# Making half of the modulated channels directly in the tile of token combinations, moving their hi/lo splits ahead of the first convolutions, and a third weight buffer in the modulation (trunk layer, float32, one core)

## The chip, the cores and the metric

The kernel runs on one core of a Trainium2 chip. The metric is the device time of one execution in microseconds (us), as the median of several runs; lower is better.

## The reference

One trunk layer on 128 prompt tokens and 512 sample tokens with 1024 channels, all float32: a modulated RMSNorm, two groups of attention heads, an output projection, a second modulated RMSNorm, and a ConvFFN with 2816 hidden channels in each of a gate and a value half. Modulation vectors come from `adaln`. What matters here is the part behind attention:

```python
sh1, sc1, gt1, sh2, sc2, gt2 = jnp.split(jax.nn.silu(cond) @ w_mod + b_mod, 6)
x = x + gt1 * rmsnorm(merge_heads(oa, ob, g_grp_a, g_grp_b, w_out), g_mix_post)
h = rmsnorm(x, g_ffn_pre) * (1 + sc2) + sh2          # modulate
u = h @ w_up                                          # 1024 -> 2 * 2816
u = up[:-2]*conv_w[0] + up[1:-1]*conv_w[1] + up[2:]*conv_w[2] + conv_b   # along tokens, zero padded
gate, val = jnp.split(u, 2)
x = x + gt2 * rmsnorm((silu(gate) * val) @ w_down, g_ffn_post)
```

## The kernel before

Float32 products are made from pairs of reduced values: every operand is split into a high part (a copy on ScalarE, `act`) and a low part (a subtraction, usually on VectorE), and `mm3` issues three matmuls for each pair of blocks. The names used below: PE is TensorE, DVE is VectorE, ACT is ScalarE, POOL is GpSimd, SP is the queue from which nearly all transfers are issued.

The kernel's instructions are issued in the order of the program text from the point on that this case is about (`manual_schedule`), each engine takes its own instructions strictly in that order, and semaphores hold an instruction until its inputs and its buffer are there. So an instruction that waits holds up everything behind it on its engine. Three stages matter.

**Projection and second norm (340 to 406 us).** Five token tiles t (t = 0 is the prompt) are projected in two halves (`p_mm`, PSUM tile `psyb`), added to the first head group (`p_y`), squared (`p_sq`), scaled by the gate (`p_z`: half 0 on POOL, half 1 on DVE), normed (`p_r`, `p_x`), squared again (`p_sx`, whose reciprocal root is two tiny POOL instructions, `rx1v` and `rx1r`), scaled (`p_n`, DVE, which makes `xn`), transposed on PE (`p_T`, PSUM `psh`), and modulated (`p_h`) into a float32 tile `hf` of 4 channel blocks by 128 tokens, one for each half `kb` of the channels; `p_s` splits it into `h2H` and `h2L`. Between them `tick` places eight small products for the last gate (`psada`, 16 matmuls each): `side_next` loads a 512 KB weight block `wms` for each, into one of two buffers (`WS`) that are used in turn. Then `up_mm(fi, gv, ch)` multiplies the hidden-channel blocks fi = 0 and 1 (gv: gate or value) with the first half of the tokens (`C1`, ch 0); `up_ev` copies the result out of PSUM into `raw`.

**Token combinations.** The later hidden blocks use a seven-product scheme over two halves of the tokens (C1, C2) and of the channels. It needs sums and differences of the modulated activations. Two tiles, `FG[0]` = F and `FG[1]` = G (both are called `fg` in the profile), are made by `fg(t)` on POOL: F = `h2H[0]` + `h2L[0]`, G = `h2H[1]` + `h2L[1]`, then G -= F. Later F and G are combined over the halves C1 and C2 on POOL and split by `t_hl` into `TF` and `TG` (`tf`, `tg` in the profile): ACT makes the high part and DVE the low part.

**Plain blocks and the unit loop (406 us on).** PSUM is handed over to four tiles of two banks: `zx` and `yy`, two buffers each. Blocks 0 and 1 get their second token half (`zz[0]`, `zz[1]`), blocks 2 and 3 are multiplied plainly (`plain`, with weights split by `plain_w`), `gate(0)` and `gate(1)` transpose the gate columns, `conv`, `silu` and `gate_mul` finish a block. Then `unit(u)` runs for u = 4 to 21, with seven products each; unit 4 needs the `zx` buffer that `conv(2, 0)` reads.

Lines of the helpers: L108 `act`, L111 `tt`, L120 `stt`, L127 `mm`; L371 `ada_mm`.

Of the kernel before, what the change touches and what calls it, by code (L numbers as in the profile page):

```python
# [15 lines left out]
KD = 8  # L16
# [10 lines left out]
def trunk_kernel(  # L27
# [46 lines left out]
    def U(shape, name, dt=F32):  # L74
        return up_.tile(shape, dt, tag="u", name=name)
# [8 lines left out]
    def PB(shape, name, dt=F32):  # L84
        return pp_.tile(shape, dt, tag="p", name=name)
# [18 lines left out]
    def f(ap):  # L104
        return ap.bitcast(F32)
# [4 lines left out]
    def tt(out, a, b, op, eng=None):  # L110
        return (eng or nc.vector).tensor_tensor(out=out, in0=a, in1=b, op=op)  # L111
# [1246 lines left out]
    def p_T(t):  # L1358
        for kb in range(2):
            pt = PS("t", "psh2")  # L1360
            hf = PB([128, 512], "h2f").rearrange("p (k t) -> p k t", k=4)
            hfs[t, kb] = pt, hf
            for kk in range(4):
                k = kb * 4 + kk
                nc.tensor.transpose(pt[:, kk * 128:kk * 128 + 128], xns[t][:, k * 128:k * 128 + 128], ident)
# [18 lines left out]
            act(h_, hv)  # L1384

    def fg_start():
        for kb in range(2):
            t_ = U([128, 4, 644], f"fg{kb}")
            FG.append(t_)
            for o, n in ((128, 1), (641, 3)):  # L1390
                nc.gpsimd.memset(t_[:, :, o:o + n], 0.0)

    def fg(t):

        c_ = slice(TO[t], TO[t] + 128)
        f_, g_ = (x[:, :, c_] for x in FG)
        for x, kb in ((f_, 0), (g_, 1)):
            tt(x, f(h2H[kb][:, :, c_]), f(h2L[kb][:, :, c_]), ALU.add, eng=nc.gpsimd)
        tt(g_, g_, f_, ALU.subtract, eng=nc.gpsimd)

    R = {}
# [89 lines left out]
    def side_next():  # L1491
        for x in sides:
            if x[1] is None:
                x[1] = WS([128, KD, 128], "wms")
                nc.sync.dma_start(
                    out=x[1], in_=wmod[:, x[0] * 128:x[0] * 128 + 128].rearrange("(k p) f -> p k f", p=128))
                return

    tn = [0]

    def tick():
        tn[0] += 1
# [8 lines left out]

    side_next()
    side_next()

    def p_hs(t):
        p_h(t, 0, range(4))
# [1 line left out]
        p_s(t, 0, 0)  # L1518
        p_s(t, 0, 1)

    p_mm(0, 0)
    p_y(0, 0)
    p_sq(0, 0)
    p_z(0, 0)
    for t in range(5):
# [33 lines left out]
        if t > 0:  # L1559
            p_hs(t - 1)  # L1560
            if t == 3:
                p_hl1(t - 1)
        p_sq(t + 1, 0)
        tick()
        p_sx(t)
        if t > 2:
            tick()
        p_z(t + 1, 0)
        if t == 2:
            load_x(4)  # L1570
    up_w(1, 0, True, 1)
# [17 lines left out]
    while act_sides:  # L1589
        tick()  # L1590
    r_load(2)
    fg_start()
    for t in range(3):
        fg(t)
    up_ev(0, 0, 0)
    p_T(4)
    p_hs(4)
    p_hl1(4)
    fg(3)
    p_s(4, 1, 1)  # L1600
    up_ev(0, 1, 0)
    up_mm(1, 1, 0)
    fg(4)
    up_ev(1, 0, 0)
    up_ev(1, 1, 0)
    r_load(3)

# [204 lines left out]
        up_mm(0, gv, 1, zz[0][:, (LS, RS)[gv]])  # L1812
    tt(F_[:, :, C2], F_[:, :, C2], F_[:, :, C1], ALU.subtract, eng=POOL)
    r_load(4)
    plain_w(2, 1)
    plain_w(3, 0)
    gate(0)
    for gv in range(2):
        up_mm(1, gv, 1, zz[1][:, (LS, RS)[gv]])
        up_ev(0, gv, 1)  # L1820
    t_hl(TG, G_, C2)
    tt(F_[:, :, C1], F_[:, :, C1], G_[:, :, C2], ALU.add, eng=POOL)
    tt(G_[:, :, C1], G_[:, :, C1], G_[:, :, C2], ALU.subtract, eng=POOL)
    for gv in (1, 0):
        conv(0, gv)
    plain(2, 0)
    for gv in range(2):
        up_ev(1, gv, 1)
    silu(0)
    gate_mul(0)  # L1830
    sums(4)
    plain_w(3, 1)
    r_load(5)
    t_hl(TF, F_, C2)
    for gv in (1, 0):
        conv(1, gv)
    gate(1)
    plain(2, 1)
    silu(1)
    gate_mul(1)  # L1840
    t_hl(TF, F_, C1)
    plain(3, 0)
    sums(5)
    t_hl(TG, G_, C1)
    a_hi(4)
    a_lo(4)
    r_load(6)
    sa_hi(4)
    sa_lo(4)
    conv(2, 0)  # L1850
    conv(2, 1)
    silu(2)
    gate_mul(2)
# [146 lines left out]
```

## Time and profile before

| | |
|---|---|
| median of 3 runs | 848.97 us |
| the 3 runs | 848.97, 855.26, 848.74 us |
| the profiled execution, its own time | 855.52 us |
| its span, first to last instruction | 853.6 us |
| PE busy / weight load busy | 806.5 us (94%) / 708.5 us (83%) |
| DVE, ACT, POOL busy | 564.7, 436.0, 303.2 us |
| mean granted PE clock | 0.976 |
| transfers | 106.59 MB, mean 125 GB/s |

All times of rows are microseconds from the start of the span. PE carries the kernel, so what is read from the profile is where PE does not work (its waits and what ended them) and where it works at a lower granted clock. Both can be seen in views of the trace: the waits of PE by what released them, the instructions of an engine in order of time, and tables of short stretches with each engine's busy time, the granted clock (PEclk, 1.00 is full) and the transfers' share. The profiled execution is 6.55 us slower than the median run.

### The profile page before, as it was taken

Reading aid. Unit: us, or ns where it says so; the run is one execution under the profiler, and the core shown is the slowest. Engines: PE = TensorE matmul, PEld = TensorE weight load, DVE = VectorE, ACT = ScalarE, POOL = GpSimd, SP = SyncE. Lnnn points to the kernel's source line nnn. Section 1 sums busy time; section 2 is a strip of 40 time slices with the busy share of each in tenths; the row PEclk is TensorE's granted clock in tenths of the full one; section 3 lists DMA queues with packets and bytes.
Section 4 is the critical chain, followed back from the end, with each engine's and each line's share of the span. In section 5 each row is a group of like instructions: output and inputs, shape, how many; then the busy total and the mean of one; then the engine's idle time right before and its main releaser. Section 6 shows DMA issues by size and latency. Waiting matters only on the chain.

```text
span 853.6 us, 13902 instructions
## 1 busy us (share of the span) xinstructions
PE 806.5 (94%) x5304; PEld 708.5 (83%) x5304; DVE 564.7 (66%) x1023; ACT 436.0 (51%) x876; POOL 303.2 (36%) x352
## 2 busy tenths in 40 slices
PE   6999989899999999989997999999999999999996
PEld 5679778788777777768997999999999987888885
DVE  3455555555888875676679899898898864332115
ACT  5345665645667886465445545546456544332112
POOL 3452333323221211346964466575575200000002
PEclk8999999999999999999998999999999999999999
DMA  9954535436312113567124243233332436434313
GB/s 290 277 142 127 155 97 142 122 105 164 86 50 75 50 51 104 197 207 196 42 65 128 83 129 110 87 115 104 107 115 84 125 114 221 171 110 161 114 50 124
DMA packets 140158, 106.59 MB, mean 125 GB/s; under 512 B 12560, under 2 KB 121388, under 8 KB 140092
## 3 DMA queue, kind: packets, MB, share of 16 engines
q1 hardware_dynamic: 139084, 105.05, 41.5%
q8 instruction: 42, 0.69, 0.4%
q10 hardware_dynamic: 1008, 0.66, 0.3%
q14 instruction: 24, 0.20, 0.1%
HBM read 92.53 MB, written 13.16 MB: 124 GB/s over the span
## 4 chain that ended last, share of the span: by engine, by line
PE 48%; DVE 28%; ACT 7%; DMA 5%; issue 4%; POOL 4%; SPq 1%; DVEq 0%; ACTq 0%; POOLq 0%
PE psd L127 16%; PE psg L127 8%; DVE cv L120 7%; DVE ou L111 5%; PE psv L127 4%; DVE cv L111 3%; DVE owl L111 3%; PE zx L127 3%; POOL fg L111 3%; PE psya L127 3%; PE psyb L127 2%; DMA wms<-in_w_mod_dram 2%; PE psS L127 2%; ACT cv L108 2%; DVE yy L111 2%
## 5 line engine op out<-in xcount | busy, mean ns | idle before, releaser
L127 PE MATMUL psd<-dwh,a 128*128 128x512 f32 x440 | 138.3, 395 | 0.0
L111 POOL TENSOR_TENSOR wsum<-wraw 128x512 f32<-128x512 f32 x36 | 77.2, 2166 | 96.9 <-DVE oc L111 89.1
L127 PE MATMUL zx<-h2H,ou 128*128 128x322 f32 x392 | 96.7, 316 | 7.5 <-DVE cv L120 4.4
L127 PEld LDWEIGHTS psd<-dwh,a 128*128 128x128 f32 x440 | 82.9, 188 | 19.7
L127 PE MATMUL psd<-dwl,a 128*128 128x512 f32 x220 | 87.1, 396 | 0.1
L111 DVE TENSOR_TENSOR dwl<-wd,dwh 128x1024 fp32r<-128x1024 f32 x22 | 26.9, 1224 | 86.7 <-ACT dwh L108 86.7
L127 PE MATMUL psg<-hH,wh 128*128 128x320 f32 x224 | 76.0, 339 | 4.4 <-ACT T L108 4.2
L127 PEld LDWEIGHTS zx<-h2H,ou 128*128 128x128 f32 x392 | 69.0, 192 | 9.9 <-DVE yy L111 5.2
L127 PE MATMUL psg<-hH,wl 128*128 128x320 f32 x224 | 70.5, 315 | 0.0
L127 PE MATMUL psg<-hL,wh 128*128 128x320 f32 x224 | 70.3, 314 | 0.0
L108 ACT ACTIVATE dwh<-wd 128x1024 fp32r<-128x1024 f32 x22 | 23.3, 1060 | 91.4 <-PE psd L127 85.7
L117 POOL TENSOR_SCALAR rdv<-ssdc 128x1 f32<-128x1 f32 x5 | 1.6, 329 | 177.3 <-ACT jk L108 177.3
L127 PE MATMUL zx<-h2L,ou 128*128 128x322 f32 x196 | 61.4, 313 | 0.0
L127 PEld LDWEIGHTS psg<-hH,wh 128*128 128x128 f32 x224 | 42.8, 191 | 13.2 <-ACT T L108 7.9
L108 ACT ACTIVATE cv<-yy,T 128x642 f32<-128x642 f32 x20 | 17.7, 886 | 66.1 <-DVE yy L111 66.1
L127 PEld LDWEIGHTS psd<-dwl,a 128*128 128x128 f32 x220 | 41.3, 188 | 10.4 <-DVE dwl L111 0.6
L111 POOL TENSOR_TENSOR wl<-wst,wh 128x1024 fp32r<-128x1024 f32 (+1 forms) x12 | 27.7, 2311 | 58.5 <-ACT wh L108 41.7
L120 DVE SCALAR_TENSOR_TENSOR cv<-yy,T,cv 128x641 f32<-128x641 f32 x40 | 35.4, 884 | 17.9 <-ACT cv L108 17.2
L108 ACT ACTIVATE P<-P,nm 128x320 f32<-128x320 f32 (+3 forms) x64 | 40.3, 630 | 7.0 <-DVE nm L626 6.9
L127 PEld LDWEIGHTS psg<-hL,wh 128*128 128x128 f32 x224 | 43.1, 192 | 0.5
L127 PEld LDWEIGHTS psg<-hH,wl 128*128 128x128 f32 x224 | 42.9, 192 | 0.0
L108 ACT ACTIVATE cv<-cv 128x642 f32<-128x642 f32 x22 | 16.4, 744 | 50.2 <-DVE cv L120 50.2
(354 smaller groups left out, 2248.0 us busy)
## 6 DMA issues: line engine op xcount, KB each, us to landing
wraw<-in_w_up_dram SPq DMA_DIRECT2D x40, 512.0 KB
wms<-in_w_mod_dram SPq DMA_DIRECT2D x32, 512.0 KB
wd<-in_w_down_dram SPq DMA_DIRECT2D x22, 512.0 KB
wm<-in_w_mod_dram SPq DMA_DIRECT2D x16, 512.0 KB
aD<-cv SPq DMA_DIRECT2D x22, 321.0 KB
ar<-aD SPq DMA_DIRECT2D x11, 642.0 KB
wst<-in_w_in_dram SPq DMA_DIRECT2D x10, 512.0 KB
yD<-Y SPq DMA_DIRECT2D x5, 512.0 KB
```

The lines of the kernel that those rows point to most:

```text
L108: return nc.scalar.activation(out=out, in_=in_, func=func, **kw)
L111: return (eng or nc.vector).tensor_tensor(out=out, in0=a, in1=b, op=op)
L117: return e.tensor_scalar(out=out, in0=a, scalar1=s1, scalar2=s2, op0=op0, op1=op1)
L120: return nc.vector.scalar_tensor_tensor(out=out, in0=a, scalar=s, in1=b, op0=op0, op1=op1)
L127: return nc.tensor.matmul(out, l, r, start=start, stop=stop, skip_group_check=True, **kw)
```

## The change

1. `p_T` lets `p_h` write its result `hf` straight into F (for kb = 0, all five t) and into G (for kb = 1, t = 3 and 4, since G exists from there on). `fg(t)` then no longer makes F, and makes the sum for G only for t < 3. The subtraction G -= F stays for all five.
2. `fg_start` makes one tile at a time: F ahead of the first `p_mm`, G ahead of `p_T(3)`. `fg(0)` is issued behind `p_n(4)`, `fg(1)` to `fg(3)` where `fg(0)` to `fg(2)` were, `fg(4)` behind the last `p_s`.
3. Every third `wms` block goes to a third buffer, the first 1024 columns of `wmsk`, which is free by then; three blocks are loaded ahead instead of two.
4. `p_z(t + 1, 0)` (POOL) is issued ahead of `p_sx(t)`.
5. `up_ev(0, 1, 0)` and `up_ev(1, 0, 0)` are issued ahead of `p_T(4)` instead of behind the last `p_s`.
6. The four `t_hl` and two of the POOL combinations are issued earlier, `conv(2, 0)` ahead of `sums(5)` and the splits of unit 4's `OSA`, `plain_w(3, 1)` behind `conv(1, ...)`.

```diff
     def p_T(t):
         for kb in range(2):
             pt = PS("t", "psh2")
-            hf = PB([128, 512], "h2f").rearrange("p (k t) -> p k t", k=4)
+            if kb < len(FG):
+                hf = FG[kb][:, :, TO[t]:TO[t] + 128]
+            else:
+                hf = PB([128, 512], "h2f").rearrange("p (k t) -> p k t", k=4)
...
     def fg_start():
-        for kb in range(2):
-            t_ = U([128, 4, 644], f"fg{kb}")
-            FG.append(t_)
...
+        t_ = U([128, 4, 644], f"fg{len(FG)}")
+        FG.append(t_)
...
     def fg(t):
...
-        for x, kb in ((f_, 0), (g_, 1)):
-            tt(x, f(h2H[kb][:, :, c_]), f(h2L[kb][:, :, c_]), ALU.add, eng=nc.gpsimd)
+        if t < 3:
+            tt(g_, f(h2H[1][:, :, c_]), f(h2L[1][:, :, c_]), ALU.add, eng=nc.gpsimd)
         tt(g_, g_, f_, ALU.subtract, eng=nc.gpsimd)
...
-                x[1] = WS([128, KD, 128], "wms")
+                sn[0] += 1
+
+                x[1] = (wmsk[:, 0:1024].rearrange("p (k f) -> p k f", k=KD) if sn[0] % 3 == 0
+                        else WS([128, KD, 128], "wms"))
...
     side_next()
     side_next()
+    side_next()
...
+    fg_start()
     p_mm(0, 0)
...
         p_sq(t + 1, 0)
+        p_z(t + 1, 0)
         tick()
         p_sx(t)
         if t > 2:
             tick()
-        p_z(t + 1, 0)
...
+    fg_start()
     p_T(3)
     p_n(4)
+    fg(0)
...
-    fg_start()
-    for t in range(3):
+    for t in range(1, 4):
         fg(t)
     up_ev(0, 0, 0)
+    up_ev(0, 1, 0)
+    up_ev(1, 0, 0)
     p_T(4)
     p_hs(4)
     p_hl1(4)
-    fg(3)
     p_s(4, 1, 1)
-    up_ev(0, 1, 0)
+    fg(4)
     up_mm(1, 1, 0)
-    fg(4)
-    up_ev(1, 0, 0)
     up_ev(1, 1, 0)
...
     r_load(4)
+    t_hl(TG, G_, C2)
     plain_w(2, 1)
+    tt(F_[:, :, C1], F_[:, :, C1], G_[:, :, C2], ALU.add, eng=POOL)
+    tt(G_[:, :, C1], G_[:, :, C1], G_[:, :, C2], ALU.subtract, eng=POOL)
+    t_hl(TF, F_, C2)
     plain_w(3, 0)
...
-    t_hl(TG, G_, C2)
-    tt(F_[:, :, C1], F_[:, :, C1], G_[:, :, C2], ALU.add, eng=POOL)
-    tt(G_[:, :, C1], G_[:, :, C1], G_[:, :, C2], ALU.subtract, eng=POOL)
     for gv in (1, 0):
         conv(0, gv)
+    t_hl(TF, F_, C1)
     plain(2, 0)
...
-    plain_w(3, 1)
     r_load(5)
-    t_hl(TF, F_, C2)
+    t_hl(TG, G_, C1)
     for gv in (1, 0):
         conv(1, gv)
+    plain_w(3, 1)
...
-    t_hl(TF, F_, C1)
-    plain(3, 0)
-    sums(5)
-    t_hl(TG, G_, C1)
     a_hi(4)
     a_lo(4)
+    plain(3, 0)
+    conv(2, 0)
+    sums(5)
     r_load(6)
     sa_hi(4)
     sa_lo(4)
-    conv(2, 0)
     conv(2, 1)
```

PE's own sequence is the same in both kernels, word for word, except that the third and the sixth of the eight `psada` groups read `wmsk`. The other engines' sequences change at these places.

On SP, from the second to the last of the `wms` loads (`xr` are the residual inputs, `yD` is where the normed rows are parked):

```order
-L1495 DMA wms<-in_w_mod_dram 128x8x128
+L1501 DMA wms<-in_w_mod_dram 128x8x128
+L1501 DMA wmsk<-in_w_mod_dram 128x8x128
 L1351 DMA yD<-Y_3916 128x1024
-L1495 DMA wms<-in_w_mod_dram 128x8x128 x2
+L1501 DMA wms<-in_w_mod_dram 128x8x128 x2
 L1351 DMA yD<-Y_3916 128x1024
-L1495 DMA wms<-in_w_mod_dram 128x8x128
+L1501 DMA wmsk<-in_w_mod_dram 128x8x128
 L1303 DMA xr<-in_x_sample_dram 128x1024
-L1495 DMA wms<-in_w_mod_dram 128x8x128
+L1501 DMA wms<-in_w_mod_dram 128x8x128
```

The third load now stands ahead of the first `yD`, and from there on each load waits for the `psada` group three before its own, instead of two before.

On ACT, at the hand-over of PSUM to `zx` and `yy`, from the first copy out of `psu` to the first weight split of the plain blocks, before:

```order
L108 ACTIVATE raw<-psu 128x322
L108 ACTIVATE h2f<-psh_5070,S_104,G_103 128x128 x4
L108 ACTIVATE h2H_4437<-h2f 128x4x128
L108 ACTIVATE h2f<-psh_5076,S_104,G_103 128x128 x2
L108 ACTIVATE h2H_4438<-h2f 128x4x128
L108 ACTIVATE raw<-psu 128x322
L108 ACTIVATE raw_5127<-psu 128x322 x2
L108 ACTIVATE ou<-wraw 128x1024
L108 ACTIVATE pwh<-wraw 128x1024
```

and in the changed kernel (`fg_4496` is F, `fg_4987` is G):

```order
L108 ACTIVATE raw<-psu 128x322 x2
L108 ACTIVATE raw_5063<-psu 128x322
L108 ACTIVATE fg_4496<-psh_5065,S_104,G_103 128x128 x4
L108 ACTIVATE h2H_4437<-fg_4496 128x4x128
L108 ACTIVATE fg_4987<-psh_5070,S_104,G_103 128x128 x2
L108 ACTIVATE h2H_4438<-fg_4987 128x4x128
L108 ACTIVATE raw_5063<-psu 128x322
L108 ACTIVATE ou<-wraw 128x1024
L108 ACTIVATE tg_5129<-fg_4987 128x4x322
L108 ACTIVATE pwh<-wraw 128x1024
```

One copy instead of three stands behind the last modulation, and the first split of G stands ahead of `pwh`.

On DVE, up to the convolution of block 2 that stands ahead of unit 4 (`cv<-raw` are the convolutions of blocks 0 and 1, `cv<-zx` is `conv(2, 0)`, `ou` and `owl` are splits of unit 4's weights), before:

```order
L111 TENSOR_TENSOR tg_5146<-fg_5056,tg_5145 128x4x322
L120 SCALAR_TENSOR_TENSOR cv<-raw,T_99,cv 128x641 x4
L111 TENSOR_TENSOR cv<-cv 128x642
L111 TENSOR_TENSOR pwl<-wraw,pwh 128x1024
L111 TENSOR_TENSOR tf_5144<-fg_5053,tf_5143 128x4x322
L120 SCALAR_TENSOR_TENSOR cv<-raw_5127,T_99,cv 128x641 x4
L111 TENSOR_TENSOR cv<-cv 128x642
L111 TENSOR_TENSOR tf_5144<-fg_5053,tf_5143 128x4x322
L111 TENSOR_TENSOR tg_5146<-fg_5056,tg_5145 128x4x322
L111 TENSOR_TENSOR ou<-wraw,ou 128x1024
L111 TENSOR_TENSOR owl<-wsum,owh 128x1024
L120 SCALAR_TENSOR_TENSOR cv<-zx,T_99,cv 128x641 x2
```

and in the changed kernel, where the first split of G (`tg`) stands right ahead of the first of these rows:

```order
L111 TENSOR_TENSOR pwl<-wraw,pwh 128x1024
L111 TENSOR_TENSOR tf_5128<-fg_4496,tf_5127 128x4x322
L111 TENSOR_TENSOR pws<-wraw,pws 128x1024
L120 SCALAR_TENSOR_TENSOR cv<-raw,T_99,cv 128x641 x4
L111 TENSOR_TENSOR tf_5128<-fg_4496,tf_5127 128x4x322
L111 TENSOR_TENSOR cv<-cv 128x642
L111 TENSOR_TENSOR tg_5130<-fg_4987,tg_5129 128x4x322
L120 SCALAR_TENSOR_TENSOR cv<-raw_5063,T_99,cv 128x641 x4
L111 TENSOR_TENSOR pwl<-wraw,pwh 128x1024
L111 TENSOR_TENSOR cv<-cv 128x642
L111 TENSOR_TENSOR ou<-wraw,ou 128x1024
L120 SCALAR_TENSOR_TENSOR cv<-zx,T_99,cv 128x641 x2
```

The splits of F and G that stood right ahead of unit 4's weights now stand among the convolutions of blocks 0 and 1, and between those and `conv(2, 0)` only two weight splits and a product are left.

More of the change, by code (lines that the diff above doesn't have):

```diff
@@ L1386, in fg_start @@
     def fg_start():
-        for kb in range(2):
-            t_ = U([128, 4, 644], f"fg{kb}")
-            FG.append(t_)
-            for o, n in ((128, 1), (641, 3)):
-                nc.gpsimd.memset(t_[:, :, o:o + n], 0.0)
+        t_ = U([128, 4, 644], f"fg{len(FG)}")
+        FG.append(t_)
+        for o, n in ((128, 1), (641, 3)):
+            nc.gpsimd.memset(t_[:, :, o:o + n], 0.0)
     def fg(t):
@@ L1497, in side_next @@
                 return
-    tn = [0]
+    tn, sn = [0], [0]
     def tick():
```

## The prediction

> **What bounds the kernel now.** I read the page first, and its first part says where to look:
>
> ```profile
> PE 806.5 (94%) x5304; PEld 708.5 (83%) x5304; DVE 564.7 (66%) x1023; ACT 436.0 (51%) x876; POOL 303.2 (36%) x352
> ```
>
> PE is the bound, and PE's own sequence of instructions does not change. So the change can only be worth what PE waits, or runs at a reduced clock, in the stretch that it touches. The view of PE's waits, asked for 330 to 460 us, has four rows in all:
>
> ```profile
> PE zx L127 <- DVE cv L120: 4.4, 1, 4.4
> PE psada L371 <- DMA wms<-in_w_mod_dram: 2.9, 1, 2.9
> PE zx L127 <- ACT raw L108: 2.2, 1, 2.2
> PE psh L1365 <- DVE xn L116: 1.7, 1, 1.7
> ```
>
> Together 11.2 us. The second thing is the clock. The table of short stretches shows it around these waits (the third number from the end is the granted clock):
>
> ```profile
> 355.00:359.00 4.00, 2.26 (x20) 1.56 (x22) 2.74 (x3) 0.86 (x4) 3.42 (x5) 1.00 0.02 4
> 379.00:380.00 1.00, 0.00 (x0) 0.00 (x0) 0.42 (x2) 1.00 (x3) 0.00 (x0) 0.92 1.02 295
> 386.00:387.00 1.00, 1.00 (x5) 0.80 (x4) 0.00 (x0) 0.00 (x0) 0.00 (x0) 0.66 0.00 0
> 407.00:408.00 1.00, 1.00 (x7) 1.00 (x6) 0.62 (x1) 0.35 (x1) 0.94 (x1) 0.58 1.15 288
> 410.00:411.00 1.00, 1.00 (x7) 1.00 (x6) 0.00 (x0) 0.00 (x0) 1.00 (x2) 0.72 0.00 0
> 454.00:455.00 1.00, 0.00 (x0) 0.00 (x0) 1.00 (x1) 0.00 (x0) 0.00 (x0) 0.97 0.14 39
> 461.00:462.00 1.00, 1.00 (x6) 1.00 (x5) 0.63 (x2) 1.00 (x2) 0.00 (x0) 0.62 0.22 82
> ```
>
> Between full speed and 0.50, a mean of 0.92 is 0.16 us at half, 0.66 is 0.68 us, and so on. So the clock was 0.50 from 379.84 to 386.68, from 407.16 to 410.56 and from 454.94 to 461.76: 6.84, 3.40 and 6.82 us, that is two, one and two pieces of some 3.41 us, and the starts lie 8 and 14 such pieces apart (27.32 and 47.78 us). The clock is decided piece by piece, and a piece that PE mostly waited through costs speed in the next. The wait of 1.7 us near 357 us cost none (1.00).
>
> **The change, term by term**, all against the profiled execution's own 855.52 us (the span and 1.92 us around it).
>
> *The third buffer.* PE's instructions in order of time at the second wait, and SP's loads ahead of it:
>
> ```profile
> 372.65 3.07 PE L127 MATMUL psyb<-wo,ob 128*128 128x512 f32 x12
> 377.10 0.85 PE L835 MATMUL psada<-sel,m 128*128 128x2 f32 x4
> 380.90 1.08 PE L371 MATMUL psada<-wms,cpad 128*32 128x128 f32 x16 [2.95 <-DMA wms<-in_w_mod_dram]
> 381.91 5.22 PE L127 MATMUL psyb<-wo,ob 128*128 128x512 f32 x12
> ...
> 371.43 0.37 SPq L1495 DMA_DIRECT2D wms<-in_w_mod_dram  x1
> 371.85 0.57 SPq L1351 DMA_DIRECT2D yD<-Y  x1
> 372.78 4.81 SPq L1495 DMA_DIRECT2D wms<-in_w_mod_dram  x2
> ```
>
> The seventh load was issued at 372.78, behind the sixth and a `yD` store, and PE got it at 380.90: 8.1 us. PE reached it at 377.95. In the changed kernel the seventh waits for the fourth `psada` group (which let the sixth go at 371.43 before) and the sixth for the third. So it goes 1.35 us sooner relative to PE, ahead of that store, and with the sixth issued one group earlier too. The sixth load, issued at 371.43, was used by the matmuls just ahead of 377.10, some 5 us later; issued at that time the seventh is there by 376.5, before 377.95. I take the whole wait as gone, 2.95 us. With it goes the slow piece: PE came back at 380.90 and the clock at 386.68, 5.78 us at half speed, 2.9 us lost (the same 12 matmuls took 5.22 instead of 3.07 us). Together **5.8 us**, bounds 0 and 5.8. The added early load goes out behind the inputs that are needed first, and nothing reads it before the third `psada` group, so its 512 KB are hidden by the first two tiles' projections.
>
> *p_z ahead of p_sx.* The first transposes waited for `xn` of tile 0:
>
> ```profile
> 353.00 0.64 ACT L108 ACTIVATE jk<-Y 128x512 f32<-128x512 f32 x1 [3.66 <-DVE Y L120]
> ...
> 356.02 1.75 DVE L116 TENSOR_SCALAR xn<-Y,rx1r 128x1024 f32<-128x1024 f32 x1
> 365.14 0.75 DVE L116 TENSOR_SCALAR xn<-Y,rx1r 128x1024 f32<-128x1024 f32 x1
> 354.87 0.30 POOL L117 TENSOR_SCALAR rx1v<-ssy,cst 128x1 f32<-128x1 f32 x1 [3.97 <-ACT xn L108]
> 355.79 1.43 POOL L111 TENSOR_TENSOR Y<-Y,gga 128x512 f32<-128x512 f32 x1
> ```
>
> POOL's 1.43 us product lay beside that `xn`, which took 1.75 us where the next took 0.75. It may start when ACT's square has read its input, at 353.6, so ahead of `rx1v` it ends near 355.1. `rx1v` and `rx1r` took 0.9 us together (354.87 to 355.79), so they end near 356.0, and `xn` starts as before but runs alone: **0.9 us**. Bounds: 0 (the reciprocal root becomes late instead) and 1.7.
>
> *The copies out of PSUM.* PE finished `up_mm(1, 1, 0)` at 404.29 (406.46 less the wait of 2.17) and could start on `zx` when ACT had emptied its bank:
>
> ```profile
> 403.95 0.81 ACT L108 ACTIVATE h2f<-psh,S,G 128x128 f32<-128x128 f32 x2 [1.45 <-DVE h2f L117]
> 404.79 0.63 ACT L108 ACTIVATE h2H<-h2f 128x512 fp32r<-128x512 f32 x1
> 405.32 1.08 ACT L108 ACTIVATE raw<-psu 128x322 f32<-128x322 f32 x3
> 406.46 0.41 PE L127 MATMUL zx<-h2H,wh 128*128 128x322 f32 x1 [2.17 <-ACT raw L108]
> ```
>
> One copy is left there, about 0.42 of the 1.08 us, so PE starts 0.66 us earlier; the other two move into ACT's idle 1.45 us and cost nothing while that lasts, 0.66 us if it is gone. What remains is the modulation of the last tile, which waits for DVE, with POOL's additions beside it as before. (That `hf` now lies in rows of a 644 wide tile I cost at nothing: ACT's copy into `h2H`, laid out like that, took 0.63 us, its square into a plain tile of that size 0.64 in the rows further up. DVE's subtraction already wrote such a tile.) A wait of 1.5 us is less than the 1.7 us that kept the full clock, so I take the slow piece as gone: 3.40 us at half, 1.7 us. Together **2.4 us**; bounds 0, and 3.4 if only one copy's time is left.
>
> *F made directly, splits earlier.* The last wait, at 452.59, is for `conv(2, 0)` on DVE, which stood behind a queue without a gap:
>
> ```profile
> 448.02 2.32 DVE L111 TENSOR_TENSOR tf<-fg,tf 128x1288 fp32r<-128x1288 f32 x1 [0.20 <-ACT tf L108]
> 450.25 2.59 DVE L111 TENSOR_TENSOR tg<-fg,tg 128x1288 fp32r<-128x1288 f32 x1
> 452.77 1.21 DVE L111 TENSOR_TENSOR ou<-wraw,ou 128x1024 fp32r<-128x1024 f32 x1
> ...
> 455.04 1.79 DVE L120 SCALAR_TENSOR_TENSOR cv<-zx,T,cv 128x641 f32<-128x641 f32 x2
> ```
>
> That DVE is late here comes from the start of the stage: it stood idle 3.8 us for `pwh` and 3.9 us for `tg`, which ACT could not make before POOL had finished G:
>
> ```profile
> 405.45 1.34 DVE L111 TENSOR_TENSOR h2L<-h2f,h2H 128x512 fp32r<-128x512 f32 x1 [0.34 <-ACT h2H L108]
> ...
> 412.79 2.36 DVE L111 TENSOR_TENSOR pwl<-wraw,pwh 128x1024 fp32r<-128x1024 f32 x1 [3.76 <-ACT pwh L108]
> 421.25 2.56 DVE L111 TENSOR_TENSOR tg<-fg,tg 128x1288 fp32r<-128x1288 f32 x1 [3.89 <-ACT tg L108]
> L111 POOL TENSOR_TENSOR fg<-h2H,h2L 128x512 f32<-128x512 f32 x10 | 17.0, 1725 | 0.0
> L111 POOL TENSOR_TENSOR fg<-fg,fg 128x512 f32<-128x512 f32 x5 | 8.2, 1644 | 0.4
> 406.46:456.98 50.52, 46.13 (x304) 45.87 (x305) 36.63 (x24) 21.66 (x26) 36.72 (x19) 0.95 0.25 67
> ```
>
> POOL keeps 3 of the 10 additions and the 5 subtractions: 7 x 1.73 = 12.1 us less. G's last subtraction must wait for DVE's last low part, 405.45 + 1.34 = 406.8, so it ends near 408.4 instead of near 420 (the start of `tg`, less 1.3 us for ACT). ACT then makes its half of `tg` by 409.8. Behind it on ACT wait `pwh`, `pws` and the copies that free `zz[0]`; PE needs that buffer 104 matmuls after the first on `zx`, at 46.13 / 304 = 0.15 us each 15 us later, so they may come that late. On DVE `tg` starts at 409.8, 4 us behind PE's first `zx` matmul, now at 405.8. The last row above has all of DVE's work of this stretch, 36.6 us; if all of it came behind 409.8, without gaps and slowed by POOL as before, it would end at 446.4. PE arrives 46.1 - 1.7 us after 405.8, at 450.2. So the wait goes, with 4 us for gaps on DVE to spare: 4.4 us, and the half-speed piece from 456.98 to 461.76, 2.4 us. **6.8 us**, bounds 0 and 6.8.
>
> *The sum.* 5.8 + 0.9 + 2.4 + 6.8 = 15.9 us, so 855.52 - 15.9 = 839.6. After these, PE runs into the next wait only in the unit loop, which has it already.
>
> Against the median, 848.97, a choice is needed: the profiled execution is 6.55 us slower, and the page does not show why. If nothing of that lies in these waits, the median run comes to 848.97 - 15.9 = 833.1. If it is the slow pieces behind the two shorter waits (2.9 and 1.7 us, which hang on where the pieces of 3.41 us fall) and one more slow piece elsewhere (1.7 us), 6.3 us in all, the change gains 15.9 - 4.6 = 11.3 us there: 837.7. I take **838**, beside which 839.6 also lies.
>
> The Trainium skill, in "TensorE: Matmul & The Clock Gate", section "Why this matters for your kernels", says that the clock falls back only over idle gaps of more than about 3 us. By it the waits of 2.95 and 2.17 us cost no speed, and the sum is 11.3 us instead of 15.9, 844.2 against 855.52. The trace disagrees: the clock was 0.50 after both.
>
> **The rivals.** *The copies still come late* (0.15): ACT's last modulation hangs on DVE, and DVE on POOL, whose 1.7 us additions lie beside it as before. For it speaks that ACT already waited 1.45 us for DVE; against it, that no work is added on either. With the 2.4 and the 0.9 lost, 12.6 us are left: 842.9.
>
> *The third buffer doesn't do what it says* (0.08): the seventh load is late for a reason other than its issue, as 8.1 us for 512 KB suggests. The sixth's 5 us speaks against it. 10.1 us are left: 845.4.
>
> *The last wait stays* (0.08): `tg` now stands ahead of `pwh` and the PSUM copies on ACT, and waits for POOL. It decides if POOL ends G more than 4 us later than 408.4, or DVE gets gaps of that size. 9.1 us are left: 846.4.
>
> *The unit loop gets slower* (0.04), the case on the other side:
>
> ```profile
> PE zx L127 <- DVE yy L111: 4.7, 13, 0.4
> L111 DVE TENSOR_TENSOR ou<-wraw,ou 128x1024 fp32r<-128x1024 f32 x16 | 36.0, 2252 | 0.0
> ```
>
> From 462 to 690 us PE waits 0.36 us in 13 of the units, for DVE. This split takes 2.25 us there on the mean, and 1.21 at 452.77 above; if DVE, now early, falls beside POOL's sums with one more instruction, each of 18 units can lose 1.0 us: 839.6 + 18 = 857.6. It is slower than before once a unit loses 0.9 us (15.9 / 18). Against it: DVE came late into the loop before and still caught up within three units.
>
> **How the numbers follow.** Forecast 0.60 (833 to 840.5), the rivals 0.15, 0.08, 0.08 and 0.04, and 0.05 for a new wait that I don't see. About 1% of 848.97, 8.5 us, is what a measurement here can tell from no change; it lies at 840.5. Below it are nearly all of the forecast and, for a run like the median, some of the cases with one term lost: 0.68 faster. The slower side is the unit loop alone, 0.04; 0.28 lie within 1%. The range 832 to 846 takes in the sum at both starting points and the cases with one term lost.
>
> **What would show it.** Right: in the profile after, PE's waits between 330 and 460 us are near 2.5 us in sum, none for `wms` or for `cv`; POOL's `fg` additions count 3; `tg` starts on DVE within some 7 us of PE's first `zx` matmul (before, 14.8); the clock stays 1.00 from 345 us into the unit loop. Wrong: a wait for ACT before plain block 2 (`zx`), a `wms` load still over 6 us under way while PE stands, or waits above 0.5 us for `yy` in the units.

## The result, and the profile after

The changed kernel takes 837.94 us (median of 4 runs, 835.72 to 842.98); the kernel before beside it 848.86 us (847.29 to 855.26). The ratio is **0.9853, 95% interval 0.9816 to 0.9891**. The profiled execution took 835.72 us, its span is 833.8 us. The first part of the page, PE's waits between 330 and 460 us, and the table of two neighbouring pieces of 3.41 us (PE busy first, the granted clock third from the end), all of the changed kernel:

```profile
PE 798.2 (96%) x5304; PEld 701.1 (84%) x5304; DVE 564.8 (68%) x1023; ACT 435.2 (52%) x876; POOL 294.2 (35%) x345
```

```profile
PE zx L127 <- ACT raw L108: 2.1, 1, 2.1
PE psh L1368 <- DVE xn L116: 1.3, 1, 1.3
```

```profile
389.71:393.12 3.41, 1.42 (x10) 1.16 (x8) 3.06 (x5) 2.30 (x6) 3.33 (x3) 1.00 1.17 290
393.12:396.53 3.41, 3.32 (x12) 3.33 (x13) 2.23 (x2) 0.98 (x2) 2.75 (x2) 0.50 0.69 173
```

Two of the four waits are gone, those for `wms` and for `cv`. The one for `xn` went from 1.74 to 1.30 us, the one for `raw` only from 2.17 to 2.08, and half speed still follows it. Where the two profiled executions differ, counted between the first instructions of PE on each tile:

| stretch | before | after | difference |
|---|---|---|---|
| start to the first `psyb` | 340.7 | 333.6 | -7.1 |
| first `psyb` to first `psu` | 46.3 | 40.2 | -6.0 |
| first `psu` to first `zx` | 19.5 | 19.4 | -0.1 |
| first `zx` to unit 4 | 50.5 | 45.9 | -4.6 |
| unit 4 to the first `psd` (down projection) | 235.4 | 234.0 | -1.5 |

The first line is ahead of nearly all changed code: it held six half-speed pieces before and two after. The same stretch took between 333.1 and 341.9 us in the variants below, whose instructions there differ by one early load and a few tiny `memset`s at most. So I read it as a draw of each execution, not a gain, and the change is worth what the other lines hold, some 12 us.

**How the runs are compared below.** Each run lists its time, its span and its mean clock. I call (1 - clock) x span its clock part. Over 168 runs of 12 kernels, taken within each kernel and group, a run with 1 us more of clock part took 0.80 us more (+-0.03). A time less 0.80 of the clock part scatters by 1.1 us instead of 2.4 (standard deviation), and I call it the time at full clock. Means with standard errors, the 68 runs of before beside the variants taken together:

| kernel | runs | time | clock part | at full clock |
|---|---|---|---|---|
| before | 68 | 850.9 +-0.3 | 16.0 +-0.3 | 838.05 +-0.1 |
| changed, both groups | 10 | 838.3 +-1.0 | 9.1 +-1.1 | 830.9 +-0.3 |
| third buffer alone | 12 | 848.4 +-0.6 | 15.2 +-0.7 | 836.2 +-0.4 |
| F direct and splits alone | 12 | 844.7 +-0.9 | 13.2 +-0.8 | 834.1 +-0.3 |
| changed, two buffers | 6 | 841.4 +-1.4 | 9.8 +-1.8 | 833.55 +-0.2 |
| changed, POOL's additions back | 12 | 847.9 +-0.7 | 12.8 +-0.7 | 837.55 +-0.4 |
| changed, old order of splits | 6 | 840.2 +-0.9 | 11.3 +-1.1 | 831.0 +-0.4 |
| changed, old order of copies | 6 | 840.4 +-0.7 | 11.9 +-0.7 | 830.9 +-0.6 |
| changed, `fg` behind `xn` | 6 | 840.1 +-0.7 | 11.2 +-1.0 | 831.1 +-0.2 |
| changed, no additions | 6 | 839.8 +-1.3 | 12.9 +-1.1 | 829.5 +-0.4 |
| ... and small instructions late, twice | 12 | 837.7 +-0.7 | 10.1 +-0.8 | 829.6 +-0.4 |
| before, wait filled | 12 | 851.0 +-0.7 | 15.3 +-0.8 | 838.7 +-0.5 |

The change gains 12.7 us in the mean: 7.1 at full clock and 0.80 x 6.9 = 5.5 through the clock.

### The profile page after: what moved, and what is told of

It reads as the page before. It is cut to its first block, busy times and chain, and to the rows that moved or that the text cites. A ratio compares the mean times of both kernels' runs of the same rounds, so it can differ in the third digit from the quotient of the medians.

```text
span 833.8 us, 13898 instructions
## 1 busy us (share of the span) xinstructions
PE 798.2 (96%) x5304; PEld 701.1 (84%) x5304; DVE 564.8 (68%) x1023; ACT 435.2 (52%) x876; POOL 294.2 (35%) x345
## 4 chain that ended last, share of the span: by engine, by line
PE 55%; DVE 27%; ACT 7%; issue 4%; DMA 4%; POOL 2%; SPq 0%; DVEq 0%; ACTq 0%; POOLq 0%
PE psd L127 18%; PE psg L127 9%; PE zx L127 6%; DVE ou L111 5%; DVE cv L120 5%; DVE owl L111 3%; DVE cv L111 3%; PE psya L127 3%; PE psv L127 2%; PE yy L127 2%; PE psS L127 2%; PE psyb L127 2%; PE psO L127 2%; DVE yy L111 2%; ACT cv L108 2%
## 5 line engine op out<-in xcount | busy, mean ns | idle before, releaser
L127 PEld LDWEIGHTS psg<-hH,wh 128*128 128x128 f32 x224 | 42.4, 189 | 12.7 <-ACT T L108 7.3
L120 DVE SCALAR_TENSOR_TENSOR cv<-yy,T,cv 128x641 f32<-128x641 f32 x40 | 35.4, 885 | 19.4 <-ACT cv L108 18.7
L111 DVE TENSOR_TENSOR ou<-wraw,ou 128x1024 fp32r<-128x1024 f32 x19 | 41.9, 2205 | 0.0
```

Of the source, the lines that this page charges most:

```text
L120: return nc.vector.scalar_tensor_tensor(out=out, in0=a, scalar=s, in1=b, op0=op0, op1=op1)
L127: return nc.tensor.matmul(out, l, r, start=start, stop=stop, skip_group_check=True, **kw)
```

## The experiments

**The changed kernel again**, beside its variants.

> The changed kernel once more, beside its variants on the same chip. All theories: 0.982 to 0.989 of before. Of the gain, the part at full clock (each run's time less the share of its span that the clock was short) should be 5 to 6.5 us and the rest, 3 to 7 us, the clock: before lost 16 us to it in the median of 23 runs, the changed kernel 9 in 4. If the clock's part is only chance of those 4 runs, it loses 13 us or more here and the ratio is above 0.99.

Measured: 837.41 us, ratio 0.9855 (0.9816 to 0.9894), clock part 8.8 us. The part won through the clock is no accident of the first four runs. In this execution the wait for `raw` is again 2.1 us; the pieces around it, by the same table:

```profile
389.09:392.50 3.41, 2.44 (x17) 2.18 (x15) 3.37 (x7) 2.20 (x6) 3.33 (x4) 1.00 1.16 290
392.50:395.91 3.41, 2.32 (x15) 2.33 (x16) 2.88 (x3) 1.95 (x4) 2.79 (x2) 1.00 0.96 242
395.91:399.32 3.41, 3.41 (x26) 3.41 (x24) 1.08 (x1) 2.23 (x2) 3.33 (x2) 1.00 0.02 5
```

The same kernel with the same wait, and no half speed behind it: here the wait straddles a border of two pieces, which hold 0.97 and 1.09 us of it. In the rows shown first one piece held 1.99 us.

**The third buffer alone**, on the kernel before.

```diff
-                x[1] = WS([128, KD, 128], "wms")
+                sn[0] += 1
+                x[1] = (wmsk[:, 0:1024].rearrange("p (k f) -> p k f", k=KD) if sn[0] % 3 == 0
+                        else WS([128, KD, 128], "wms"))
...
+    side_next()
```

> The kernel before with the third weight buffer and the third early load alone. Theory (the term of the prediction, 5.8 us): the wait for the seventh wms block, 2.95 us, goes, and with it the half-clock piece behind it; the waits for xn (1.7), raw (2.2) and cv (4.4) stay. PE's waits between 330 and 460 us then sum to about 8 us, and the time is 4 to 6 us below before, 0.993 to 0.996. Rival 1: only the wait goes, since a half-clock piece falls by chance: about 3 us, 0.997. Rival 2: the 7 us that the changed kernel is ahead already at its first projection come from the third early load, not from where clock pieces fall: then 7 us more, 10 to 13 us in all, 0.985 to 0.988.

Measured: ratio 0.9967 (0.9947 to 0.9988), 1.9 us at full clock. The two longest of PE's waits from 330 us to the end of the units; those for `raw` and `xn` are as before, and a new one of 0.6 us stands in plain block 3:

```profile
PE zx L127 <- DVE cv L120: 6.3, 1, 6.3
PE zx L127 <- DVE yy L111: 5.3, 14, 0.6
```

The wait for `wms` is gone, but that for `cv` grew from 4.4 to 6.3 us. Counted from the first `psyb` matmul, PE came to it 6.2 us earlier than in the profiled execution of before, which had lost time to half speed as well, and DVE only 4.3 us earlier. So part of the gain was given back 75 us later. The first rival's number came out, for a reason that neither theory had; the second fell.

**Two buffers in the changed kernel** (the same edit taken back).

> The changed kernel with two weight buffers and two early loads as before, all else as changed. Theory: the wait for the seventh wms block comes back, near 2.9 us, and a half-clock piece behind it in some runs (1.7 us): 3 to 5 us slower than the changed kernel, 0.989 to 0.992 of before. Rival: the early load is worth the 7 us ahead of the projection too: 10 us slower, 0.997.

Measured: ratio 0.9883 (0.9847 to 0.9919); at full clock 2.6 us slower than the changed kernel, nearly the whole of the returned wait:

```profile
PE psada L371 <- DMA wms<-in_w_mod_dram: 2.6, 1, 2.6
PE zx L127 <- ACT raw L108: 1.4, 1, 1.4
```

The wait for `raw` is shorter here, 1.4 us instead of 2.1. POOL's `rx1r` of the fourth tile and DVE's instructions beside and behind it show why, first in the changed kernel, then here:

```profile
375.70 0.69 DVE L111 TENSOR_TENSOR Y<-Y,gga 128x512 f32<-128x512 f32 x1 [0.90 <-ACT jk L108]
375.76 1.06 POOL L111 TENSOR_TENSOR rx1r<-rx1v,cst 128x1 f32<-128x1 f32 x1
376.85 0.76 DVE L116 TENSOR_SCALAR xn<-Y,rx1r 128x1024 f32<-128x1024 f32 x1 [0.45 <-POOL rx1r L111]
```

```profile
375.24 0.56 POOL L111 TENSOR_TENSOR rx1r<-rx1v,cst 128x1 f32<-128x1 f32 x1
377.69 0.69 DVE L111 TENSOR_TENSOR Y<-Y,gga 128x512 f32<-128x512 f32 x1 [0.79 <-ACT jk L108]
378.30 0.75 DVE L116 TENSOR_SCALAR xn<-Y,rx1r 128x1024 f32<-128x1024 f32 x1
```

PE's wait for the block delays its next projection, and with it DVE's product, so POOL finishes `rx1r` alone. Without that wait `rx1r` falls beside DVE's product and takes 1.06 us, and DVE's chain comes 0.7 us later against PE: counted from the first `psu` matmul, `xn` of the last tile starts at 8.07 us in the changed kernel and at 7.36 here. So by the traces the buffer is worth 2.6 less 0.7, 1.9 us. The runs at full clock say 2.6 +-0.4 here and 1.9 +-0.4 for the buffer alone, which is no clear difference. No half speed followed this wait of 2.6 us; its pieces held 1.06 and 1.62 us of PE's idle time.

**POOL's additions back**, orders, copies and buffer as changed.

```diff
-            if kb < len(FG):
-                hf = FG[kb][:, :, TO[t]:TO[t] + 128]
-            else:
-                hf = PB([128, 512], "h2f")...
+            hf = PB([128, 512], "h2f")...
...
-        if t < 3:
-            tt(g_, f(h2H[1][:, :, c_]), f(h2L[1][:, :, c_]), ALU.add, eng=nc.gpsimd)
+        for x, kb in ((f_, 0), (g_, 1)):
+            tt(x, f(h2H[kb][:, :, c_]), f(h2L[kb][:, :, c_]), ALU.add, eng=nc.gpsimd)
```

> The changed kernel with F and G made by POOL's additions from h2H and h2L for all five tiles, as before (hf in a buffer of its own), but with all orders, the copies and the third buffer as changed. Theory (the prediction's term): POOL's chain gets 7 instructions of 1.3 to 1.7 us more, G is finished 8 to 12 us later, tg and tf come so much later on DVE, the 4.2 us by which conv(2, 0) is ahead of unit 4 are used up, and PE waits 3 to 8 us for cv again: 3 to 9 us slower than the changed kernel, 0.989 to 0.996 of before. Rival: the order of the splits and of conv(2, 0) ahead of unit 4's own splits is what removed the wait: then POOL's relief is worth nothing, the wait stays away and the time is the changed kernel's, 0.985.

Measured: ratio 0.9961 (0.994 to 0.9982), 6.6 us slower than the changed kernel at full clock. PE's waits, POOL's group of additions, and the split of G on ACT and DVE:

```profile
PE zx L127 <- ACT raw L108: 5.0, 2, 3.2
PE yy L127 <- DVE pwl L111: 3.4, 1, 3.4
```

```profile
L111 POOL TENSOR_TENSOR fg<-h2H,h2L 128x512 f32<-128x512 f32 x10 | 15.0, 1525 | 0.0
```

```profile
405.53 1.28 ACT L108 ACTIVATE tg<-fg 128x1288 fp32r<-128x1288 f32 x1 [11.25 <-POOL fg L111]
...
406.84 2.58 DVE L111 TENSOR_TENSOR tg<-fg,tg 128x1288 fp32r<-128x1288 f32 x1 [10.22 <-ACT tg L108]
```

ACT and DVE stand 11 and 10 us for POOL. The size is as expected, the place is not: with `tg` ahead of the copies and of `pwl` in the new order, PE is late at plain blocks 2 and 3 already (3.2 us for `raw` of the second token half, 3.4 for `pwl`), and no wait for `cv` is left.

**The old order of the splits**, F still made directly.

```diff
-    t_hl(TG, G_, C2)
     plain_w(2, 1)
-    tt(F_[:, :, C1], F_[:, :, C1], G_[:, :, C2], ALU.add, eng=POOL)
-    tt(G_[:, :, C1], G_[:, :, C1], G_[:, :, C2], ALU.subtract, eng=POOL)
-    t_hl(TF, F_, C2)
     plain_w(3, 0)
...
+    t_hl(TG, G_, C2)
+    tt(F_[:, :, C1], F_[:, :, C1], G_[:, :, C2], ALU.add, eng=POOL)
+    tt(G_[:, :, C1], G_[:, :, C1], G_[:, :, C2], ALU.subtract, eng=POOL)
...
+    plain(3, 0)
+    sums(5)
+    t_hl(TG, G_, C1)
     a_hi(4)
     a_lo(4)
-    plain(3, 0)
-    conv(2, 0)
-    sums(5)
...
     sa_lo(4)
+    conv(2, 0)
```

> The changed kernel with the splits of F and G, POOL's combinations, conv(2, 0) and the splits of weights in the order of before, F still made directly, the copies and the third buffer as changed. With the run in which POOL made all additions in the new order, it tells whether order or POOL's relief took away the wait for cv. Theory (both are needed): DVE has what it needs early, but conv(2, 0) stands again behind sums(5), tg and two more splits, so PE waits for cv at unit 4, though less than the 4.4 us of before, since tg no longer holds DVE up: 1.5 to 3.5 us; at full clock 1.5 to 3.5 us slower than the changed kernel, 0.988 to 0.994 of before. Rival (POOL's relief alone did it): no wait for cv, the time of the changed kernel, 0.985.

Measured: ratio 0.9877 (0.984 to 0.9914), and 831.0 at full clock, that of the changed kernel. No wait for `cv`. `conv(2, 0)` on DVE and PE's first matmul of unit 4 in this variant:

```profile
444.24 1.79 DVE L120 SCALAR_TENSOR_TENSOR cv<-zx,T,cv 128x641 f32<-128x641 f32 x2
...
447.50 0.32 PE L127 MATMUL zx<-h2H,ou 128*128 128x322 f32 x1
```

DVE is done 1.5 us ahead of PE. My theory (both are needed) fell and the rival holds: POOL's relief did it, and the moved splits and combinations widen the margin, from 1.5 to 4.2 us. Both margins are from executions in which PE lost 1.5 us to half speed on the way to unit 4 (46.0 and 45.9 us from the first `zx`); in the second execution of the changed kernel, at full speed, it took 44.4 us and 2.35 us are left. So in the old order the margin would be near nothing at full speed, by estimate.

**F direct and the new order alone**: two buffers, `p_z` and the raw copies as before.

> The other way round: F made directly and the splits in the new order, while the weight buffers, p_z and the raw copies are those of before. Theory (the prediction's fourth term alone): the waits for wms (2.6 to 2.9) and raw (2.7) are there, none for cv; 4.4 us less at full clock than before, and about 2 us less lost to the clock: 0.991 to 0.994. With the third buffer alone at 0.997 that is nearly the whole gain, so little is left for p_z and the copies. Rival: DVE gets behind without the other edits and PE waits for cv or pwl again: 0.997 or more.

Measured: ratio 0.9932 (0.9904 to 0.996), 4.0 us at full clock, and no wait for `cv` (expected 4.4). The waits at the seventh `wms` block, 2.4 us, and for `raw`, 2.0, are there; the profile puts the first down to DVE's `h2L`, which ended in the same moment. The second is not 2.7, with the copies in their old place, since with two buffers `rx1r` is again done alone in 0.56 us and `xn` of the last tile starts 7.37 us behind the first `psu` matmul; in the next run, with three buffers, it starts at 8.06. With the 2.6 us of the third buffer, and by the traces 0.44 of `p_z` and 0.66 of the copies, the parts make 7.7 us against 7.1, which agrees within their errors of 0.3 to 0.4 each.

**The raw copies back in their old place.**

```diff
-    up_ev(0, 1, 0)
-    up_ev(1, 0, 0)
     p_T(4)
...
     fg(4)
+    up_ev(0, 1, 0)
     up_mm(1, 1, 0)
+    up_ev(1, 0, 0)
```

> The changed kernel with the two raw copies back behind the last split, ahead of and behind up_mm(1, 1, 0), as before. Theory (the prediction's term): three copies then stand between the last split and PE, so its wait for raw rises by the 0.66 us that two of them take, from 2.1 to 2.7 us, and ACT idles longer for DVE; 0.7 us slower than the changed kernel at full clock. Rival: what PE waits for is DVE's chain, whose last part ACT works off while DVE is still busy; copies in ACT's gaps cost nothing, the wait stays at 2.1 to 2.2 us, and the edit is worth nothing.

Measured: the wait, and the three copies behind the last split:

```profile
PE zx L127 <- ACT raw L108: 2.7, 1, 2.7
```

```profile
395.20 1.08 ACT L108 ACTIVATE raw<-psu 128x322 f32<-128x322 f32 x3
```

The copies cost the 0.66 us that the prediction gave them. The time (0.9883, interval 0.9851 to 0.9916; the same at full clock, +-0.7) cannot tell so small a difference; this rests on the trace.

**`fg` behind `xn`**: why the wait for `raw` stayed.

```diff
     p_n(4)
+    tt(FG[1][:, 0, 128:129], xns[4][:, 0:1], xns[4][:, 0:1], ALU.subtract, eng=nc.gpsimd)
     fg(0)
```

> The changed kernel with one more tiny POOL instruction ahead of the first fg addition: it subtracts a column of xn of the last tile from itself and writes the zero into a padding column of G, so that POOL starts its additions only when xn of the last tile is there. Theory: PE still waits 2.1 us for raw because POOL's first addition lay beside that xn and made it 1.84 us instead of 0.76; here xn takes 0.76, the chain on DVE comes about 1 us earlier and the wait for raw falls to 1.0 to 1.5 us; 1 us faster than the changed kernel, and 1.7 us more if the half-clock piece behind it goes too (0.982 to 0.985 of before). Unit 4 still finds cv in time, since fg of the last tile ends at most 1 us later of a margin of 4. Rival: the additions only move, and lie beside the next DVE instructions (wu, h2L) instead: the wait stays at 1.9 to 2.2 us and the time with the changed kernel's.

DVE's `xn` of the last tile and POOL's first additions in the kernel before:

```profile
394.34 0.76 DVE L116 TENSOR_SCALAR xn<-Y,rx1r 128x1024 f32<-128x1024 f32 x1 [1.13 <-POOL rx1r L111]
394.44 3.05 POOL L111 TENSOR_TENSOR fg<-h2H,h2L 128x512 f32<-128x512 f32 x2
```

The changed kernel, the same two, then the last modulation on both engines, the copy, and PE:

```profile
381.88 1.84 DVE L116 TENSOR_SCALAR xn<-Y,rx1r 128x1024 f32<-128x1024 f32 x1 [1.13 <-POOL rx1r L111]
381.89 1.27 POOL L111 TENSOR_TENSOR fg<-h2H,h2L 128x512 f32<-128x512 f32 x1
...
391.35 0.81 ACT L108 ACTIVATE fg<-psh,S,G 128x128 f32<-128x128 f32 x2 [1.08 <-DVE fg L117]
...
392.73 0.42 ACT L108 ACTIVATE raw<-psu 128x322 f32<-128x322 f32 x1
393.21 0.64 PE L127 MATMUL zx<-h2H,wh 128*128 128x322 f32 x1 [2.08 <-ACT raw L108]
```

And the variant:

```profile
384.14 0.75 DVE L116 TENSOR_SCALAR xn<-Y,rx1r 128x1024 f32<-128x1024 f32 x1 [1.13 <-POOL rx1r L111]
385.04 0.20 POOL L111 TENSOR_TENSOR fg<-xn 128x1 f32<-128x1 f32 x1 [0.84 <-DVE xn L116]
...
394.80 0.41 PE L127 MATMUL zx<-h2H,wh 128*128 128x322 f32 x1 [1.14 <-ACT raw L108]
```

`xn` takes 0.75 us instead of 1.84 once POOL is kept off, and the wait falls by 0.94: what POOL's addition cost the wait is shown. In the kernel before the addition lay beside `xn` as well, but began 0.10 us behind it and not 0.01, and `xn` took 0.76. The time did not follow: 0.9867 (0.9842 to 0.9893), 831.1 at full clock, unchanged. In this execution G is ready later, and PE waits 0.5 us for `pwl` in plain block 3, half of what was won.

**No additions at all**, built on that run: the second half of `hf` of tiles 0 to 2 waits in other buffers until G exists.

```diff
-                hf = PB([128, 512], "h2f")...
+                hf = (FP if t < 2 else PB)([128, 512], "h2f")...
...
-        if t < 3:
-            tt(g_, f(h2H[1][:, :, c_]), f(h2L[1][:, :, c_]), ALU.add, eng=nc.gpsimd)
-        tt(g_, g_, f_, ALU.subtract, eng=nc.gpsimd)
+        tt(g_, hfs[t, 1][1], f_, ALU.subtract, eng=nc.gpsimd)
```

> The run with the tiny instruction for xn, and besides it the last three additions of POOL taken out: the second half of hf of tiles 0 to 2 stays in buffers of its own until G exists, and one subtraction, hf less F, makes G. POOL then has five fg instructions instead of eight ahead of the sums. Theory: POOL is done with tiles 0 to 3 by about 391 us instead of 397, fg of the last tile starts when DVE has its split, tg comes on ACT and DVE some 2 us earlier than in that run, and the wait of 0.5 us for pwl goes; DVE's instructions beside POOL are fewer, so the wait for raw falls from 1.1 to 0.5 to 0.9 us. In all 1 us faster than the changed kernel at full clock, 0.5 to 1 us faster than the run it builds on. Rival: POOL is off the path since the change, so nothing moves beyond what the tiny instruction gave.

Measured: the wait for `raw` is 1.0 us (0.5 to 0.9 expected), that for `pwl` is gone, and at full clock it is 1.6 +-0.5 us faster than the run it builds on and 1.4 +-0.5 faster than the changed kernel. The ratio, 0.9878 (0.9837 to 0.992), does not show it: these six runs had a clock part of 12.9 us.

**The small instructions late**, built on that, run twice.

```diff
-    while act_sides:
-        tick()
     r_load(2)
...
     fg(4)
+    while act_sides:
+        tick()
     up_mm(1, 1, 0)
```

> The run before this one, with the small instructions that finish the last gate product on DVE (gtmp and S, 1.2 us) issued behind the last tile's modulation and splits. Theory: the wait for raw hangs on DVE's chain from xn of the last tile to h2f of the last tile; 1.2 us less in it takes that wait to about 0.5 us, which is the latency of the last copy itself: 0.3 to 0.6 us faster at full clock than the run before, and 1.5 us faster than the changed kernel (0.98 to 0.986 of before). Rival: by now PE's own matmuls or ACT's instructions end last, and it is worth nothing.

> The same kernel as the run with the small instructions behind the last tile's splits, once more, since its median of 835.9 us lay 1.5 us below that of the changed kernel with spreads of 5 and 9 us. Theory: it is faster than the changed kernel by the 1.5 us of the wait for raw and what the clock loses behind it, 2 to 3 us in all: 0.980 to 0.985 of before. Rival: the lower median was chance of where the half-clock pieces fell: 0.985 to 0.988.

Measured: ratios 0.984 (0.9806 to 0.9873) and 0.9844 (0.9814 to 0.9875). The end of the wait in the first of them:

```profile
397.65 0.41 PE L127 MATMUL zx<-h2H,wh 128*128 128x322 f32 x1 [0.64 <-ACT raw L108]
```

That is the last copy itself, 0.42 us, which now begins as soon as PE has finished. At full clock the kernel is 1.3 +-0.5 us faster than the changed one. In plain time, 837.7 +-0.7 against 838.3 +-1.0, it is not shown to be faster. Nor is it against the run that it builds on (829.6 against 829.5 at full clock), though the wait fell from 1.0 to 0.6 us. So neither theory's gain is shown, and that over the changed kernel is there without this last edit.

**The wait filled**: does PE's standing idle cause the half speed?

```diff
+    up_mm(3, 1, 1, YY[3][:, RS])
     for u in range(NP_, NF):
         unit(u)
```

> The kernel before, with 24 matmuls (3.6 us) issued twice: the last ones of plain block 3 are repeated into the same bank just ahead of unit 4, where PE waits 4.4 us for cv. This does no useful work and moves nothing else; it only fills most of the wait. Theory (a piece of 3.41 us in which PE stood idle for some 1.6 us or more makes the next one run at half clock): the wait shrinks to 0.8 us, unit 4 starts when it did, no half-clock piece follows in the profile, and the loss to the clock falls by 1.5 to 2.5 us in the mean of the runs while the rest of the time stays: 0.997 to 0.998 of before. Rival: the slow pieces have another cause (load on the chip, temperature, the start of a new stage): they stay behind unit 4's start, and the time is that of before or, if the doubled matmuls delay something, up to 3.6 us longer.

Measured: ratio 1.0008 (0.9981 to 1.0034). PE's start of unit 4; the piece in which most of the wait lay before, in the kernel before; the same piece and the next here; and PE's waits for `yy` behind unit 4's start, in the kernel before and here:

```profile
453.82 0.39 PE L127 MATMUL zx<-h2H,ou 128*128 128x322 f32 x1 [0.80 <-DVE cv L120]
```

```profile
451.53:454.94 3.41, 1.06 (x8) 0.79 (x6) 3.41 (x3) 1.07 (x2) 0.00 (x0) 1.00 0.74 211
```

```profile
452.03:455.44 3.41, 2.62 (x18) 2.38 (x18) 3.28 (x4) 1.52 (x2) 0.00 (x0) 1.00 0.00 0
455.44:458.85 3.41, 3.41 (x25) 3.41 (x24) 3.33 (x5) 2.99 (x5) 0.14 (x1) 1.00 0.25 96
```

```profile
PE zx L127 <- DVE yy L111: 5.3, 14, 0.6
```

```profile
PE zx L127 <- DVE yy L111: 6.1, 16, 0.6
```

In this execution the piece went as the theory has it: idle time of 0.8 us instead of 2.35, and full clock behind it. The worth is not. From unit 4 to the first `psd` it took 234.6 us; before, with 4.8 us of half speed in that stretch, 235.4. Only 0.8 of the 2.4 us came out. PE at full speed meets DVE earlier and waits for `yy` 16 times instead of 14, which takes back another 0.8; where the rest went the traces do not tell. The clock part (15.3 +-0.8 against 15.5 +-0.6 of the before beside it) did not fall by the expected 1.5 to 2.5 us either; why not stays open.

## Why the prediction was right or wrong

The time, 838, was right, and so were the range and the sign. By its own steps:

- **Third buffer: right in the wait.** The seventh block's matmuls follow the sixth's without a wait:

```profile
363.90 0.37 SPq L1501 DMA_DIRECT2D wms<-in_w_mod_dram  x1
...
370.35 0.65 PE L371 MATMUL psada<-wms,cpad 128*32 128x128 f32 x16
370.92 3.05 PE L127 MATMUL psyb<-wo,ob 128*128 128x512 f32 x12
```

  The whole wait is gone; taken back, it cost 2.6 us. What the prediction did not see is that this makes the wait for `raw` 0.7 us longer. The 2.9 us of half speed were those of one execution: the wait of 2.6 us in the variant had none behind it.

- **`p_z` ahead of `p_sx`: half.** The term was 0.9 us, it gave 0.44 in the traces; no run took this edit back by itself. `xn` runs alone as forecast (0.76 us), but the step "`rx1v` and `rx1r` took 0.9 us together" failed: the reciprocal root, 1.06 us, now falls beside DVE's own product.

```profile
348.32 0.69 DVE L111 TENSOR_TENSOR Y<-Y,gga 128x512 f32<-128x512 f32 x1 [1.34 <-ACT jk L108]
348.38 1.06 POOL L111 TENSOR_TENSOR rx1r<-rx1v,cst 128x1 f32<-128x1 f32 x1
349.48 0.76 DVE L116 TENSOR_SCALAR xn<-Y,rx1r 128x1024 f32<-128x1024 f32 x1 [0.46 <-POOL rx1r L111]
```

- **The copies: the mechanism right, the sum wrong.** Two copies are worth 0.66 us. The step that failed is "the modulation of the last tile, which waits for DVE, with POOL's additions beside it as before": DVE's chain to that modulation was not as before. With two `memset`s instead of four ahead of it, POOL's first addition began with `xn` of the last tile, which took 1.84 us instead of 0.76; and that `xn` began 0.7 us later against PE, through the longer `rx1r` of the tile before. Together they delayed the last modulation by 0.6 us, from 16.98 to 17.55 behind the first `psu` matmul, and took that much of the gain. Taking away either one shortens the wait: to 1.1 us with POOL kept off, to 1.4 with two buffers. So the wait stayed at 2.1 us instead of 1.5, and half speed can still follow. Of 2.4 us 0.1 came in the profiled execution. This is the first rival's event, in part at a new place.

- **F direct, splits earlier: right in the wait and in POOL's relief, which is what did it; the moves were not needed, and the clock behind the wait was worth less.** POOL is left with three additions, and `tg` starts 4.6 us behind PE's first `zx` matmul (4 forecast, 14.8 before):

```profile
L111 POOL TENSOR_TENSOR fg<-h2H,h2L 128x512 f32<-128x512 f32 x3 | 5.4, 1787 | 0.0
```

```profile
396.54 1.28 ACT L108 ACTIVATE tg<-fg 128x1288 fp32r<-128x1288 f32 x1 [2.44 <-POOL fg L111]
397.85 2.56 DVE L111 TENSOR_TENSOR tg<-fg,tg 128x1288 fp32r<-128x1288 f32 x1 [2.50 <-ACT tg L108]
...
433.16 1.79 DVE L120 SCALAR_TENSOR_TENSOR cv<-zx,T,cv 128x641 f32<-128x641 f32 x2
```

  DVE has finished at 434.95, PE came at 439.14: the 4 us to spare are there, with 1.5 of them from half speed that the sum did not have. The 2.4 us of half speed gave at most 1.5 (the last stretch of the first table) and 0.8 in the run that filled the wait, since longer waits for DVE in the units take back part of it.

- **The sum.** Waits: 8.9 us forecast; 2.95 + 0.44 + 0.09 + 4.39 = 7.9 in the traces, 7.4 after 0.5 us more for `yy` (5.3 to 5.8), and 7.1 at full clock in the runs. Clock: 7.0 forecast; the clock part fell by 6.9 in the mean, but a us of it costs 0.80 us and not 1, so 5.5 came out. Together 12.7 instead of 15.9. The total fitted because the second starting point, a run like the median with 11.3 us, was counted in; that it fitted to 0.1 us is luck. The profiled execution of before had a clock part of 20.1 us against 16.0 in the mean, so the guess that its extra time was slow pieces is borne out for the most part (0.80 x 4.1 = 3.3 us of the 4.6 by which it was above the mean).

- **The signs.** No wait for `wms` or `cv`, three additions and an early `tg` came as written. PE's waits sum to 3.4 us instead of 2.5, and the clock stayed at 1.00 only in the second execution. The wait for `yy` above 0.5 us, a sign of being wrong, is one of 0.59 us behind the last units that the kernel before has too.

## What to carry to other kernels

An engine that makes what the next stage splits (POOL here, 11.6 us of additions less) can be the cause of a wait 50 us later on another engine; writing the first result straight into the tile did what moving the splits alone could not (with the additions back, PE waited 6.6 us in the plain blocks), and the moves were not needed for it. A wait that goes can lengthen the next one on the same chain: without the wait for `wms`, that for `cv` grew by 1.9 us in one kernel and that for `raw` by 0.7 in the other. When an engine is relieved, look at what it now starts earlier, and beside whom.

## What the runs showed of the hardware

**Half speed comes in fixed pieces of 3.413 us, and most of it follows PE's idle time inside the piece ahead.** Within each of 14 traces all half-speed pieces begin at one phase, to 0.01 us. With PE's idle time taken for every piece between 30 and 815 us: of 15 pieces with 1.8 us or more (the least 1.89) all 15 were followed by half speed; of 34 with 1.5 to 1.8 us, 19; of 68 with 0.8 to 1.5 us, 5. It is not the whole rule: of the other 3089 pieces 10 were followed by half speed too, five as the second of two in a row, and five between 307 and 317 us, where the trace shows PE idle for at most 0.3 us; what caused those is not known. A wait of 2 to 3 us therefore costs by where it falls, as the two executions of the changed kernel show. The Trainium skill, in "TensorE: Matmul & The Clock Gate", section "What's actually happening", has the free-running window of 3413 ns, and the traces agree; it lets the clock fall after an idle window, where here 1.89 idle us of 3.41 were enough.

**A half-speed piece costs less than half its length**: 0.80 us for each us of clock part, so some 1.4 us for a piece of 3.41. That other engines go on meanwhile, and that PE waits for some of that time anyway, is the likely reason; no run tests it.

**DVE's scaling of 128x1024 takes 0.75 us alone, 1.84 beside one POOL addition that starts with it, and 0.76 beside one that starts 0.10 us later.** The Trainium skill, in "SBUF — State Buffer", section "Who interferes with whom", says that `tensor_scalar` can contend with GpSimd and that the order of issue decides who is blocked; the rows of that experiment agree, though 0.01 us between the two starts is too little to tell which was issued first.
